# PSUM buffers of a score kernel re-dealt: shared in the first unit, one engine each, two-bank transposed tiles from the third unit on

## The chip, the cores and the metric

The kernel runs on one core of a Trainium2 chip. The metric is the device time of one execution in microseconds (us), taken as the median of several runs; lower is better. Engines are called PE (matmul), PEld (weight load, beside PE), DVE (vector), ACT (scalar), POOL (GpSimd) and SP (which here only issues transfers).

## The reference

```python
def setup_inputs():
    batch, heads, seq, dim = 8, 8, 512, 64      # q and k: float32, 16.8 MB together

def reference(q, k):
    scale = 1.0 / np.sqrt(q.shape[-1])
    return (np.einsum('bhqd,bhkd->bhqk', q, k) * scale).astype(np.float32)   # 67.1 MB
```

The output is four times the input. The matmuls contract over 64 only.

## The kernel before

The work is cut into four units of two batches each. A unit is loaded (two DMAs of 2.1 MB), cast to bf16 on POOL, transposed on PE into PSUM (the memory that PE writes to here), and copied out of PSUM by DVE and ACT into `kT` and `qz`, the operands of the score matmuls. Then 32 pairs of score matmuls follow, each into a PSUM tile of 4 KB per partition, which is scaled into one of the large SBUF buffers. (A tile of 4 KB per partition is called two-bank here, one of 2 KB one-bank.) Eight such scalings, called evacuations, fill one buffer, and one DMA of 4.19 MB stores it: 16 stores in all. The three large buffers (`big`) serve the loads and the stores alike. While unit v is scored, the transposes and copies of unit v+1 are taken in small steps between the evacuations; a step is the transposes of one tile, or one copy. Every engine runs its instructions in this program order.

```python
    big_pool = ctx.enter_context(tc.tile_pool(name="big", bufs=3))
    bf_pool = ctx.enter_context(tc.tile_pool(name="bf", bufs=6))
    tpsum_pool = ctx.enter_context(tc.tile_pool(name="tpsum", bufs=2, space=bass.MemoryType.PSUM))
    psum_pool = ctx.enter_context(tc.tile_pool(name="psum", bufs=3, space=bass.MemoryType.PSUM))
    # [cut]
    def evacuate(dst, src):
        nonlocal n_evac
        if n_evac % 6 in (0, 2, 3):
            pinned(nc.scalar.mul(out=dst, in_=src, mul=scale))
        else:
            pinned(nc.vector.tensor_scalar(out=dst, in0=src, scalar1=scale, scalar2=None,
                                           op0=mybir.AluOpType.mult))
        n_evac += 1

    def rearrange(tp, pattern, dst):          # four copies of one transposed tile
        nonlocal n_tp
        copy = (nc.vector.tensor_copy, nc.scalar.copy)[n_tp % 2]
        n_tp += 1
        for s in range(2):
            src = tp[half(s)].rearrange(pattern, n=N, h=2)
            for h in range(2):
                pinned(copy(out=dst(s, h), in_=src[:, h]))
                yield

    def transpose(v, kb, qb):
        # [cut]
        for j0 in range(0, J, 8):             # four tiles of k; four more of q follow alike
            tp = tpsum_pool.tile([P, 8, P], bf16, name="tp")
            for j in range(8):
                pinned(nc.tensor.transpose(out=tp[:, j, :], identity=identity,
                                           in_=kb[:, j0 + j].rearrange("p s d -> p (s d)")))
            yield
            yield from rearrange(tp, "d j (n h m) -> d h n m j",
                                 lambda s, h: kT[half(h), :, :, s, j0:j0 + 8])
    # [cut]
    for v in range(UNITS):
        ahead = transpose(v + 1, *cast[v + 1]) if v + 1 < UNITS else iter(())
        for t in range(TILES):
            for n, _ in enumerate(scores(v, t)):
                take(ahead, 1 + (t > 0 if v == 0 else n % 4 == 3))
```

Of the kernel before, what the change touches and what calls it, by code (L numbers as in the profile page):

```python
# [1 line left out]

# [5 lines left out]


@with_exitstack  # L10
def kernel(
    ctx: ExitStack,
    tc: tile.TileContext,
    q: bass.AP,
    k: bass.AP,
    out: bass.AP,
):






    nc = tc.nc
    B, H, S, D = q.shape
    scale = 1.0 / (D ** 0.5)
    P = 128
    UNITS = B // 2
    N = H
    M = P // (2 * H)  # L30
    R = S // M
    J = R // 2
    RO = 8
    U = S // RO
    JJ = J // RO
    IW = 8 // JJ
    TILES = N // 2

    f32 = mybir.dt.float32
    bf16 = mybir.dt.bfloat16  # L40

    q_r = q.rearrange("(v b) g (m j) d -> v (b g m) (j d)", b=2, j=R)
    k_r = k.rearrange("(v b) g (m j) d -> v (b g m) (j d)", b=2, j=R)
    out_r = out.rearrange("(v b) (t x h) (u i) k -> v (b t) (h u) x (i k)", b=2, x=2, h=2, i=RO)

    consts = ctx.enter_context(tc.tile_pool(name="consts", bufs=1))

    big_pool = ctx.enter_context(tc.tile_pool(name="big", bufs=3))
    bf_pool = ctx.enter_context(tc.tile_pool(name="bf", bufs=6))
    t_pool = ctx.enter_context(tc.tile_pool(name="t", bufs=2))  # L50
    tpsum_pool = ctx.enter_context(tc.tile_pool(name="tpsum", bufs=2, space=bass.MemoryType.PSUM))
    psum_pool = ctx.enter_context(tc.tile_pool(name="psum", bufs=3, space=bass.MemoryType.PSUM))


    pinned = tc.keep_in_program_order

    n_evac = 0
    n_tp = 0

    def evacuate(dst, src):  # L60
        nonlocal n_evac

        if n_evac % 6 in (0, 2, 3):
            pinned(nc.scalar.mul(out=dst, in_=src, mul=scale))  # L64
        else:
            pinned(nc.vector.tensor_scalar(out=dst, in0=src, scalar1=scale, scalar2=None,  # L66
                                           op0=mybir.AluOpType.mult))
        n_evac += 1

    def half(h):  # L70
        return slice(h * D, (h + 1) * D)

    def load_and_cast(v):

        xf = big_pool.tile([P, 2, 2, J * D], f32, name="big")
        both = []
        for x, src in enumerate((k_r, q_r)):
            nc.sync.dma_start(out=xf[:, x], in_=src[v].rearrange("p (s c) -> p s c", s=2))  # L78
        for x in range(2):
            xb = bf_pool.tile([P, J, 2, D], bf16, name="xb")  # L80
            for s in range(2):
                pinned(nc.gpsimd.tensor_copy(out=xb[:, :, s, :],  # L82
                                             in_=xf[:, x, s].rearrange("p (j d) -> p j d", j=J)))
            both.append(xb)
        return both

    def rearrange(tp, pattern, dst):
# [10 lines that stand above are left out]
    def transpose(v, kb, qb):  # L98


        kT = t_pool.tile([P, N, M, 2, J], bf16, name="kT")
        qz = qzs[v % 2]
        ts[v] = (kT, qz)
        for j0 in range(0, J, 8):
            tp = tpsum_pool.tile([P, 8, P], bf16, name="tp")
            for j in range(8):
                pinned(nc.tensor.transpose(out=tp[:, j, :], identity=identity,  # L107
                                           in_=kb[:, j0 + j].rearrange("p s d -> p (s d)")))
            yield
            yield from rearrange(tp, "d j (n h m) -> d h n m j",  # L110
                                 lambda s, h: kT[half(h), :, :, s, j0:j0 + 8])
        for i0 in range(0, RO, IW):
            tp = tpsum_pool.tile([P, IW, JJ, P], bf16, name="tp")
            for i in range(IW):
                for jj in range(JJ):
                    pinned(nc.tensor.transpose(out=tp[:, i, jj, :], identity=identity,  # L116
                                               in_=qb[:, RO * jj + i0 + i].rearrange("p s d -> p (s d)")))
            yield
            yield from rearrange(tp, "d i jj (n h m) -> d h i n m jj",
                                 lambda s, h: qz[half(h), i0:i0 + IW, :, h * U:(h + 1) * U]  # L120
                                 .rearrange("d i n (m s jj) -> d s i n m jj", s=2, jj=JJ)[:, s])

    def scores(v, t):

        kT, qz = ts[v]
        o = big_pool.tile([P, 2, RO, S], f32, name="big")
        for x in range(2):
            n = 2 * t + x
            for i in range(0, RO, 2):
                ps = psum_pool.tile([P, 2, S], f32, name="ps")  # L130
                for w in range(2):
                    pinned(nc.tensor.matmul(out=ps[:, w, :], lhsT=qz[:, i + w, n, :],  # L132
                                            rhs=kT[:, n].rearrange("d m s j -> d (m s j)"),
                                            start=True, stop=True))
                evacuate(o[:, x, i:i + 2, :], ps)
                yield
        nc.sync.dma_start(out=out_r[v, t], in_=o.rearrange("p x i k -> p x (i k)"))  # L137

    def take(steps, count):
        for _ in range(count):  # L140
            next(steps, None)

    identity = consts.tile([P, P], dtype=bf16)
    make_identity(nc, identity)
    qzs = [consts.tile([P, RO, N, P], bf16, name=f"qz{n}") for n in range(2)]
    for qz in qzs:
        nc.vector.memset(qz, 0.0)  # L147
    cast = [load_and_cast(v) for v in range(UNITS)]

    ts = {}  # L150
    for _ in transpose(0, *cast[0]):
        pass
    for v in range(UNITS):
        ahead = transpose(v + 1, *cast[v + 1]) if v + 1 < UNITS else iter(())
        for t in range(TILES):
            for n, _ in enumerate(scores(v, t)):

                take(ahead, 1 + (t > 0 if v == 0 else n % 4 == 3))
        for _ in ahead:
            pass  # L160


# [1 line left out]
_INS = ['q', 'k']  # L164
_OUTS = [((8, 8, 512, 512), 'float32')]


# [23 lines left out]
```

## Time and profile before

| what | value |
|---|---|
| time, median of the first 3 runs | 202.97 us (202.87 to 203.42) |
| span of the profiled run | 201.3 us |
| busy PE, DVE, ACT, POOL | 99.2, 126.4, 100.7, 30.6 us |
| bytes moved | 83.97 MB |

"Busy" is an engine's own working time. Those shares are averages over the whole span and do not say what bounds the kernel. The slices and windows do, and they are shown and read in the prediction. One idea from there is the **margin** of a store: how long before the transfer queue would run dry the store is issued. With 4.19 MB per store at 0.4295 MB/us, the queue would run dry at 41.7 us without any store, and 9.77 us later for each store issued. The margin of store number i (from 0) is 41.7 + 9.77 i (unrounded, 41.695 + 9.766 i) minus the time of its issue, read from the timeline's SP rows. While it is positive, transfers go on without a pause.

### The profile page before, as it was taken

The numbers are of one execution on the slowest core, as the hardware profiler recorded it, in microseconds if no ns is written. First come the engines' busy times: TensorE is split into PE (matmuls) and PEld (weight loads), VectorE is DVE, ScalarE is ACT, GpSimd is POOL, SyncE is SP. The second block draws the span as 40 slices with busy tenths as digits, with TensorE's granted clock in tenths as the row PEclk, the third lists the DMA queues.
The fourth block names the chain that finished last, engine by engine and source line by source line (L and its number), as shares of the span: only waits on it lengthen the run. The fifth ranks groups of instructions, "written<-read, shape, count | busy, mean of one in ns | idle before, by whom it ended". The sixth has DMA issues, their size and how long they took to land.

```text
span 201.3 us, 1456 instructions
## 1 busy us (share of the span) xinstructions
PE 99.2 (49%) x503; PEld 48.3 (24%) x512; DVE 126.4 (63%) x130; ACT 100.7 (50%) x129; POOL 30.6 (15%) x22
## 2 busy tenths in 40 slices
PE   0033366753976729463729554856535666710000
PEld 0033353321522414231315221432212222200000
DVE  6726659995989929796749796569635264530000
ACT  2016667786674856583837663856515341510000
POOL 1277777556000000000000000000000000000000
PEclk9999999998599996999975998888995857555555
DMA  6999999999999999999999999999999999999993
GB/s 205 430 443 430 420 433 440 420 407 427 433 436 425 422 443 427 430 423 440 430 423 433 433 430 427 440 430 423 433 436 430 410 446 433 420 423 433 433 427 163
DMA packets 5510, 83.97 MB, mean 417 GB/s; under 512 B 384, under 2 KB 384, under 8 KB 384
## 3 DMA queue, kind: packets, MB, share of 16 engines
q1 hardware_dynamic: 5504, 83.89, 98.1%
q8 instruction: 4, 0.07, 0.1%
q14 instruction: 2, 0.02, 0.0%
HBM read 16.78 MB, written 67.11 MB: 417 GB/s over the span
## 4 chain that ended last, share of the span: by engine, by line
DMA 63%; DVE 16%; PE 3%; POOL 3%; ACT 1%; POOLq 1%; issue 1%; SPq 0%; DVEq 0%; ACTq 0%
DMA out_dram<-big 43%; DMA big<-in_q_dram 20%; DVE big L66 12%; PE ps L132 3%; DVE qz L95 3%; POOL xb L82 3%; DVE kT L95 1%; ACT big L64 1%; POOLq L186 1%; SPq L78 0%; DVEq L66 0%; SPq L137 0%; ACTq L64 0%; POOLq L82 0%
## 5 line engine op out<-in xcount | busy, mean ns | idle before, releaser
L132 PE MATMUL ps<-kT,qz 128*128 128x512 bf16 x247 | 81.1, 450 | 55.1 <-ACT big L64 39.2
L66 DVE TENSOR_SCALAR big<-ps 128x1024 f32<-128x1024 f32 x64 | 76.3, 1222 | 39.9 <-DMA out_dram<-big 29.1
L64 ACT ACTIVATE big<-ps 128x1024 f32<-128x1024 f32 x64 | 63.7, 1023 | 57.0 <-DMA out_dram<-big 30.8
L132 PEld LDWEIGHTS <-qz 128*128 128x128 bf16 x256 | 27.5, 111 | 96.0 <-issue 83.2
L82 POOL CAST xb<-big 128x2048 bf16<-128x2048 f32 x16 | 29.9, 1896 | 17.6 <-DMA big<-in_k_dram 11.9
L95 DVE COPY kT<-tp 64x512 bf16<-64x512 bf16 x32 | 22.0, 687 | 6.3 <-PE tp L107 5.7
L95 ACT COPY kT<-tp 64x512 bf16<-64x512 bf16 x32 | 18.5, 578 | 14.7 <-PE tp L107 14.4
L95 DVE COPY qz<-tp 64x512 bf16<-64x512 bf16 x32 | 22.0, 687 | 3.1 <-PE tp L116 2.7
L95 ACT COPY qz<-tp 64x512 bf16<-64x512 bf16 x32 | 18.5, 578 | 3.9 <-PE tp L116 3.6
L107 PE MATMUL tp<-identity,xb 128*128 128x128 bf16 x128 | 12.0, 254 | 16.5 <-POOL xb L82 12.5
L116 PE MATMUL tp<-identity,xb 128*128 128x128 bf16 x128 | 12.8, 265 | 6.0 <-DVE kT L95 3.5
L107 PEld LDWEIGHTS <-xb 128*128 128x128 bf16 x128 | 10.5, 116 | 20.8 <-POOL xb L82 12.8
L116 PEld LDWEIGHTS <-xb 128*128 128x128 bf16 x128 | 11.3, 122 | 10.9 <-issue 8.9
L147 DVE MEMSET qz<- 128x4096 uint32 x2 | 6.9, 3472 | 2.5 <-PEq L175 1.7
L95 ACT ACT_TABLE_LOAD x1 | 1.3, 1283 | 0.7 <-PEq L175 0.7
masks.py:199 POOL TENSOR_SCALAR_AFFINE_SELECT identity<-identity 128x128 bf16<-128x128 bf16 x1 | 0.3, 294 | 0.1
masks.py:197 POOL MEMSET identity<- 128x128 bf16 x1 | 0.2, 205 | 0.3 <-POOLq L175 0.3
L175 POOL MEMSET const-float32-0.0<- 128x1 f32 x1 | 0.1, 99 | 0.2 <-issue 0.2
L175 POOL MEMSET const-bfloat16-1.0<- 128x1 bf16 x1 | 0.1, 102 | 0.0
L175 POOL MEMSET const-uint8-127<- 128x1 uint8 x1 | 0.1, 102 | 0.0
L175 POOL MEMSET const-float32-1.0<- 128x1 f32 x1 | 0.1, 99 | 0.0
## 6 DMA issues: line engine op xcount, KB each, us to landing
out_dram<-big SPq DMA_DIRECT2D x16, 4096.0 KB, 21.4
big<-in_k_dram SPq DMA_DIRECT2D x4, 2048.0 KB, 19.2
big<-in_q_dram SPq DMA_DIRECT2D x4, 2048.0 KB, 24.2
```

The source lines that it names most:

```text
L64: pinned(nc.scalar.mul(out=dst, in_=src, mul=scale))
L66: pinned(nc.vector.tensor_scalar(out=dst, in0=src, scalar1=scale, scalar2=None, op0=mybir.AluOpType.mult))
L82: pinned(nc.gpsimd.tensor_copy(out=xb[:, :, s, :], in_=xf[:, x, s].rearrange("p (j d) -> p j d", j=J)))
L95: pinned(copy(out=dst(s, h), in_=src[:, h]))
L107: pinned(nc.tensor.transpose(out=tp[:, j, :], identity=identity, in_=kb[:, j0 + j].rearrange("p s d -> p (s d)")))
L116: pinned(nc.tensor.transpose(out=tp[:, i, jj, :], identity=identity, in_=qb[:, RO * jj + i0 + i].rearrange("p s d -> p (s d)")))
L132: pinned(nc.tensor.matmul(out=ps[:, w, :], lhsT=qz[:, i + w, n, :], rhs=kT[:, n].rearrange("d m s j -> d (m s j)"), start=True, stop=True))
L147: nc.vector.memset(qz, 0.0)
L175: nc = _bacc.Bacc("TRN2", target_bir_lowering=False, num_devices=1)
L186: with _tile.TileContext(nc) as tc:
```

## The change

Its intent is to keep the compute engines moving. In the first unit, nothing is scored yet, so the transposes may also use the score tiles' PSUM. The evacuations go two to ACT and one to DVE, so that with three score tiles each PSUM buffer belongs to one engine. From the third unit on, a transposed tile is a two-bank one (16 transposes, copies of twice the length), and one of them takes the room of two. One cast moves from POOL to DVE. The step counts of the preparation change to match.

```diff
-        if n_evac % 6 in (0, 2, 3):
+        if n_evac % 3 < 2:
             pinned(nc.scalar.mul(out=dst, in_=src, mul=scale))
...
-                pinned(nc.gpsimd.tensor_copy(out=xb[:, :, s, :], ...
+                copy = nc.vector.tensor_copy if v == x == s == 0 else nc.gpsimd.tensor_copy
+                pinned(copy(out=xb[:, :, s, :], ...
...
+        W = 8 if v < 2 else 16
+        def transposed(rows):
+            if v == 0 and n_tp % 4 > 1:
+                tp = psum_pool.tile([P, W, P], bf16, name="ps")
+            else:
+                tp = tpsum_pool.tile([P, W, P], bf16, name="tp")
+            for w, row in enumerate(rows):
+                pinned(nc.tensor.transpose(out=tp[:, w, :], identity=identity, ...
+            return tp
-        for j0 in range(0, J, 8):
-            tp = tpsum_pool.tile([P, 8, P], bf16, name="tp")
+        for j0 in range(0, J, W):
+            tp = transposed([kb[:, j0 + j] for j in range(W)])
...
-                take(ahead, 1 + (t > 0 if v == 0 else n % 4 == 3))
+                take(ahead, 2 if v == 0 else n == 0 or n % 2)
...
+        if v == 0:
+            tpsum_pool = tp_pool(1)          # closes the pool of two one-bank tiles
```

(Cut: `tp_pool`, which opens the pool of two one-bank tiles and later the pool of one two-bank tile, and q's transposes, which change as k's do.)

More of the change, by code (lines that the diff above doesn't have):

```diff
@@ L35 @@
     JJ = J // RO
-    IW = 8 // JJ
     TILES = N // 2
@@ L50, with tp_pool @@
     t_pool = ctx.enter_context(tc.tile_pool(name="t", bufs=2))
-    tpsum_pool = ctx.enter_context(tc.tile_pool(name="tpsum", bufs=2, space=bass.MemoryType.PSUM))
     psum_pool = ctx.enter_context(tc.tile_pool(name="psum", bufs=3, space=bass.MemoryType.PSUM))
+    tp_pools = ctx.enter_context(ExitStack())
+    def tp_pool(bufs):
+        tp_pools.close()
+        return tp_pools.enter_context(tc.tile_pool(name=f"tpsum{bufs}", bufs=bufs, space=bass.MemoryType.PSUM))
     pinned = tc.keep_in_program_order
@@ L81, in load_and_cast @@
             for s in range(2):
-                pinned(nc.gpsimd.tensor_copy(out=xb[:, :, s, :],
-                                             in_=xf[:, x, s].rearrange("p (j d) -> p j d", j=J)))
+                copy = nc.vector.tensor_copy if v == x == s == 0 else nc.gpsimd.tensor_copy
+                pinned(copy(out=xb[:, :, s, :], in_=xf[:, x, s].rearrange("p (j d) -> p j d", j=J)))
             both.append(xb)
@@ L103, in transpose @@
         ts[v] = (kT, qz)
-        for j0 in range(0, J, 8):
-            tp = tpsum_pool.tile([P, 8, P], bf16, name="tp")
-            for j in range(8):
-                pinned(nc.tensor.transpose(out=tp[:, j, :], identity=identity,
-                                           in_=kb[:, j0 + j].rearrange("p s d -> p (s d)")))
+        W = 8 if v < 2 else 16
[5 more added lines that the diff above has]
+            for w, row in enumerate(rows):
+                pinned(nc.tensor.transpose(out=tp[:, w, :], identity=identity,
+                                           in_=row.rearrange("p s d -> p (s d)")))
+            return tp
+        for j0 in range(0, J, W):
+            tp = transposed([kb[:, j0 + j] for j in range(W)])
             yield
             yield from rearrange(tp, "d j (n h m) -> d h n m j",
-                                 lambda s, h: kT[half(h), :, :, s, j0:j0 + 8])
+                                 lambda s, h: kT[half(h), :, :, s, j0:j0 + W])
+        IW = W // JJ
         for i0 in range(0, RO, IW):
-            tp = tpsum_pool.tile([P, IW, JJ, P], bf16, name="tp")
-            for i in range(IW):
-                for jj in range(JJ):
-                    pinned(nc.tensor.transpose(out=tp[:, i, jj, :], identity=identity,
-                                               in_=qb[:, RO * jj + i0 + i].rearrange("p s d -> p (s d)")))
+            tp = transposed([qb[:, RO * jj + i0 + i] for i in range(IW) for jj in range(JJ)])
             yield
-            yield from rearrange(tp, "d i jj (n h m) -> d h i n m jj",
+            yield from rearrange(tp.rearrange("p (i jj) c -> p i jj c", jj=JJ),
+                                 "d i jj (n h m) -> d h i n m jj",
                                  lambda s, h: qz[half(h), i0:i0 + IW, :, h * U:(h + 1) * U]
@@ L147 @@
         nc.vector.memset(qz, 0.0)
+    tpsum_pool = tp_pool(2)
     cast = [load_and_cast(v) for v in range(UNITS)]
```

## The prediction

> **What bounds the kernel now.** I read the page's slices first, because they tell whether any one resource is full for the whole span, and then stretches of 4 us from the table of windows.
>
> ```profile
> DMA  6999999999999999999999999999999999999993
> GB/s 205 430 443 430 420 433 440 420 407 427 433 436 425 422 443 427 430 423 440 430 423 433 433 430 427 440 430 423 433 436 430 410 446 433 420 423 433 433 427 163
> HBM read 16.78 MB, written 67.11 MB: 417 GB/s over the span
> ```
>
> The 16 DMA engines are busy in every slice but the first and the last, and they move 407 to 446 GB/s in each of the 38 between. No compute engine comes near: DVE is busy 63% of the span, ACT 50%, PE 49%. The windows (length, busy time of PE, PEld, DVE, ACT and POOL, clock, DMA share, GB/s) show the two ends, the join of the loads and the stores, and a stretch with no compute:
>
> ```profile
> 0.00:4.00 4.00, 0.00 (x0) 0.00 (x0) 2.34 (x1) 1.28 (x1) 0.70 (x6) 1.00 0.57 147
> 40.00:44.00 4.00, 2.02 (x14) 1.03 (x15) 3.90 (x6) 3.36 (x6) 2.82 (x2) 1.00 1.00 406
> 184.00:188.00 4.00, 0.00 (x0) 0.00 (x0) 0.00 (x0) 0.00 (x0) 0.00 (x0) 0.50 1.00 426
> 188.00:192.00 4.00, 0.00 (x0) 0.00 (x0) 0.00 (x0) 0.00 (x0) 0.00 (x0) 0.50 1.00 426
> 196.00:200.00 4.00, 0.00 (x0) 0.00 (x0) 0.00 (x0) 0.00 (x0) 0.00 (x0) 0.50 0.54 229
> ```
>
> With every compute engine idle the transfers run at 426 GB/s, no faster than beside full compute. So the transfers hold themselves up. Budget: 147 GB/s over the first 4 us is 0.59 MB, 229 GB/s over the last window is 0.92 MB, and the rest of the 83.97 MB, 82.47 MB, goes in the 192 us between, at 0.4295 MB/us. Time not used for bytes at that rate: 4.0 - 0.59/0.4295 = 2.6 us at the start, 5.3 - 0.92/0.4295 = 3.2 us at the end of the 201.3 us span, and 4 x (430-406)/430 = 0.2 us at the join. Nothing else is left to win.
>
> Then the waits of the DMA queue on SP, and the chain of waits around the first outputs:
>
> ```profile
> SPq L137 <- DVE big L66: 147.9, 16, 20.0
> ...
> 46.96 1.85 POOLq L186
> 48.81 0.02 issue
> 48.84 1.23 DVE big L66
> ...
> 63.61 20.21 DMA out_dram<-big
> ```
>
> The 147.9 us look as if DVE's evacuation held the stores up. It doesn't: it is SP waiting for the next full buffer while the queue still holds earlier stores. The timeline gives the first six issues of stores at 38.23, 46.07, 58.31, 63.61, 71.19 and 83.01. At 0.4295 MB/us the 16.78 MB of loads are moved by 4 + (16.78-0.59)/0.4295 = 41.7 us, and each store of 4.19 MB lasts 9.8 us, so the queue would run dry at 41.7, 51.5, 61.3, 71.1, 80.8 and 90.6. The margins are 3.5, 5.4, 3.0, 7.5, 9.6 and 7.6 us. The last store is issued at 178.21, with transfers lasting to beyond 196. The kernel is bound by its transfers, with one thin place: the first three stores.
>
> **What the Trainium skill says.** "DMA: Bandwidth & Descriptors", section Where 436 GB/s comes from, puts the fabric's ceiling at 435 GB/s, and says that for HBM to SBUF some 358 binds. Here the trace differs from the second: 430 GB/s in the middle, so this kernel sits within about 1% of the first and has no rate left to gain. "SBUF — State Buffer", section SBUF: two separate sides, says that compute operations and transfers do not slow each other; the trace agrees (426 idle, 430 beside compute). "ScalarE: Activation LUTs", section What ACT_TABLE_LOAD costs, gives 186 ns + 0.833 ns per element with immediate scale: 1039 ns for 1024 elements, 612 for 512; the rows below have 1023 and 578, near enough. "VectorE: DVE Perf Modes", section The perf-mode tier table, has a float32 SBUF copy of 2048 elements at 1227 ns; the kernel before has no such copy on DVE, so the trace cannot confirm it.
>
> **The change part by part.** The rows that price it:
>
> ```profile
> L66 DVE TENSOR_SCALAR big<-ps 128x1024 f32<-128x1024 f32 x64 | 76.3, 1222 | 39.9 <-DMA out_dram<-big 29.1
> L64 ACT ACTIVATE big<-ps 128x1024 f32<-128x1024 f32 x64 | 63.7, 1023 | 57.0 <-DMA out_dram<-big 30.8
> L82 POOL CAST xb<-big 128x2048 bf16<-128x2048 f32 x16 | 29.9, 1896 | 17.6 <-DMA big<-in_k_dram 11.9
> L95 DVE COPY kT<-tp 64x512 bf16<-64x512 bf16 x32 | 22.0, 687 | 6.3 <-PE tp L107 5.7
> L95 ACT COPY kT<-tp 64x512 bf16<-64x512 bf16 x32 | 18.5, 578 | 14.7 <-PE tp L107 14.4
> ```
>
> *Evacuation two to one.* ACT takes 86 of the 128 evacuations and DVE 42: ACT 63.7 + 22 x 1.023 = 86.2 us, DVE 76.3 - 22 x 1.222 = 49.4 us. *Two-bank tiles.* For units three and four, 32 copies of 512 elements on each engine become 16 of 1024. I put such a copy at the evacuation's cost, 1.22 on DVE and 1.02 on ACT (estimates): DVE saves 32 x 0.687 - 16 x 1.22 = 2.5 us, ACT 32 x 0.578 - 16 x 1.02 = 2.2 us. *One cast moved* from POOL to DVE: +1.2 us on DVE (from the tier table), -1.9 on POOL. Sums: ACT 100.7 + 22.5 - 2.2 = 121 us, DVE 126.4 - 26.9 - 2.5 + 1.2 = 98 us. The fuller engine goes from 126 to 121 us; both stay far below the 194 us of transfers, so this is worth 0. Per steady unit the fuller engine had 16 x 1.222 + 16 x 0.687 = 30.5 us (DVE) and will have 21.3 x 1.023 + 8 x 1.02 = 30.0 us (ACT), against 4 x 9.8 = 39 us of stores. The margin hardly moves.
>
> *First unit.* Before, the casts of k run on POOL from 8.71 to 12.44, one after the other. Now one half runs on DVE, which finishes its memsets at 9.40, so k is ready near 11: 1.5 us sooner. q's casts end at 17.3, bound by its landing at 13.57, and stay. With four one-bank tiles instead of two, transposes no longer wait for copies: DVE stood idle 1.51 us between rounds. All k copies are out of the way by 17.5; q's four tiles need one transpose round (0.95 us) and two rounds of copies (2 x 2.79 us on DVE): 17.3 + 0.95 + 5.6 = 23.9, against 28.98 (DVE) and 29.38 (ACT) before, 5 us sooner. But the first output's buffer is a load buffer, free when unit two's casts end at 27.11. So the first evacuation moves from 29.41 to 27.2, and the first store from 38.23 to about 36. The queue holds loads until 41.7: worth 0, or a part of the 0.2 us dip.
>
> *Stores two and three.* The second must wait for unit three's casts (POOL, 36.9), the third for unit four's (48.81, set by a landing at 44.9); neither moves. Store three's filling took 58.31 - 48.84 = 9.5 us, with 16 steps of the next unit's transposes between its evacuations. The new schedule takes two steps from the first evacuation on, so 8 of the 40 are left for it: DVE has 3 evacuations and some 3 copies (5.7 us), ACT 5 and 4 (7.4 us). I expect its issue at 56.5 to 57, and the margin to grow from 3.0 to 4.5 us. It was never used up, so this too is worth 0. Sum of all parts: 0 to -0.2 us.
>
> **Rivals.** *The earlier start pays:* if transfers sat idle before the first store, its 2 us would come off whole, giving 201 us. For it: the dip to 406 GB/s. Against it: the DMA share is 1.00 there. *A new wait lets the queue run dry:* from unit three on a single two-bank tile serves all transposes, and PE works in order, so a late copy stalls the score matmuls behind it. Each round adds perhaps 16 transposes (1 to 2 us) and 4 copies (4 to 5 us); a buffer's fill might grow from 8 to 11 us. The margins of 7.5 us and more absorb that; only if a fill took 16 us would each store lose time, and three lost per unit would make 206 us or more. The ready-ahead copies make that unlikely. *ACT becomes the bound:* 121 us of work in 174 us before the last issue; against it. *Stores and loads collide more:* a first store issued at 36 shares engines with the last load, which would land later than 44.9 and delay the third store. The load is ahead in the queue, and a delay of 1 us fits in the margin: 203 us.
>
> **Range and chances.** I predict 202.9 us: 202.97 with at most 0.1 off. The three runs before spread over 0.55 us, so two kernels that are the same can differ by 0.5; the range is 202.2 to 203.6. Faster by 2% needs 4.06 us of the 6.0 us of unused transfer time, nearly all at the two ends, which no part touches: 1%. Slower by 2% needs the third store 3 + 4 us late or a lasting dry queue: 2%. Within 2%: 97%.
>
> **What would show it right or wrong.** Right: DMA slices unchanged at 9 with about 430 GB/s; ACT near 121 us, DVE near 98; first store issued near 36, third before 58; the last issue still near 178 and the tail unchanged. Single steps fail if a 1024-element copy costs more than an evacuation, or if the first evacuation does not move to 27. The prediction fails if a slice after the first shows the DMA share below 9, or if the rate itself, which I take as given, moves with the order of loads and stores.

## The result, and the profile after

| kernel | median | runs |
|---|---|---|
| before | 203.05 us | 202.87 to 203.42, 4 runs |
| after | 203.20 us | 203.06 to 203.36, 4 runs |

The ratio is 1.0005, 95% interval 0.9987 to 1.0023: the same. Ratios in this document are the mean time of one kernel's fast runs over that of the other's of the same rounds, so they are not quite the ratios of the medians. Where two experiments are compared with each other, their two ratios to the kernel before are divided.

The page of the changed kernel, the slices of the span and the two groups of evacuations:

```profile
DMA  6999999999999999999999999999999999999994
GB/s 205 432 426 436 426 429 439 423 397 426 436 437 419 434 432 423 436 436 429 419 439 432 419 436 442 423 423 436 439 397 426 445 423 419 419 423 442 432 426 182
...
L68 ACT ACTIVATE big<-ps 128x1024 f32<-128x1024 f32 x86 | 83.8, 1025 | 42.2 <-PE ps L144 18.1
...
L70 DVE TENSOR_SCALAR big<-ps 128x1024 f32<-128x1024 f32 x42 | 51.4, 1224 | 61.8 <-PE ps L144 37.8
```

The DMA row is as full as before. What has changed is the last column of the two groups, which names what ended the largest part of the engine's idle time. Before, it was the end of a store (lines in the prediction): ACT and DVE waited for a buffer to come free, which is the wait of a producer that is ahead. Now it is PE, with 18.1 of ACT's 42.2 us and 37.8 of DVE's 61.8: they wait for scores. PE's own waits between 60 and 160 us (for whom, us in total, times, longest) say why. First the kernel before:

```profile
PE ps L132 <- ACT big L64: 28.6, 18, 4.5
PE ps L132 <- DVE big L66: 9.8, 13, 2.0
PE tp L116 <- DVE kT L95: 0.3, 1, 0.3
```

and the changed kernel:

```profile
PE ps L144 <- ACT big L68: 9.4, 17, 2.6
PE ps L144 <- DVE big L70: 7.2, 13, 0.9
PE tp L117 <- DVE kT L99: 6.0, 2, 3.7
PE tp L117 <- ACT kT L99: 6.0, 2, 3.4
PE tp L117 <- DVE qz L99: 5.2, 2, 3.3
PE tp L117 <- ACT qz L99: 2.5, 1, 2.5
PE ps L144 <- ACT qz L99: 1.6, 1, 1.6
```

The transposes hardly waited before (0.3 us). Now they wait 19.7 us in seven waits of some 3 us. One such wait in the timeline of the changed kernel, inside the third unit's scores:

```profile
109.11 2.44 DVE L99 COPY kT<-tp 64x1024 bf16<-64x1024 bf16 x2
...
112.80 1.23 DVE L99 COPY kT<-tp 64x1024 bf16<-64x1024 bf16 x1
...
115.31 1.23 DVE L99 COPY kT<-tp 64x1024 bf16<-64x1024 bf16 x1
116.59 1.87 PE L117 MATMUL tp<-identity,xb 128*128 128x128 bf16 x16 [3.71 <-DVE kT L99]
...
118.25 2.77 PE L144 MATMUL ps<-kT,qz 128*128 128x512 bf16 x6
...
119.35 1.02 ACT L68 ACTIVATE big<-ps 128x1024 f32<-128x1024 f32 x1 [5.23 <-PE ps L144]
```

The last copy of the only transposed tile ends at 116.54. PE, which has waited 3.71 us for it, runs 16 transposes, then the scores that stand behind them in its order, and ACT has by then been idle for 5.23 us. What that does to the stores shows in their margins (us, stores 0 to 15):

```
store     0    1    2    3    4    5    6    7    8    9   10   11   12   13   14   15
before  3.5  5.4  2.9  7.4  9.6  7.5  8.8  9.8  7.7  9.0  8.8  7.8 11.0 10.0  9.6 10.0
after   6.5  4.4  5.1  9.2  9.0  7.8  8.1  6.0  4.5  2.3  1.5  0.6  3.7  8.5 11.3  9.9
```

The first store is issued at 35.24 us instead of 38.23, as intended, and its margin grows by 3 us. From store 6 to store 11 the issues come 11.3 us apart ((148.55 - 92.23) / 5), slower than the queue empties, and the margin falls to 0.6 us. Then the last unit, which prepares nothing, wins it back. The time did not move. Either both effects are hidden by the transfers, or two small real effects cancel.

### The profile page after: what moved, and what is told of

Its sections match the earlier page's. It is cut to its first block, busy times and chain, and to the rows that moved or that the text cites. A ratio compares the mean times of both kernels' runs of the same rounds, so it can differ in the third digit from the quotient of the medians.

```text
span 201.6 us, 1437 instructions
## 1 busy us (share of the span) xinstructions
PE 100.9 (50%) x512; PEld 49.1 (24%) x512; DVE 100.5 (50%) x93; ACT 118.7 (59%) x135; POOL 30.4 (15%) x21
## 5 line engine op out<-in xcount | busy, mean ns | idle before, releaser
L68 ACT ACTIVATE big<-ps 128x1024 f32<-128x1024 f32 x86 | 83.8, 1025 | 42.2 <-PE ps L144 18.1
L70 DVE TENSOR_SCALAR big<-ps 128x1024 f32<-128x1024 f32 x42 | 51.4, 1224 | 61.8 <-PE ps L144 37.8
L144 PEld LDWEIGHTS <-qz 128*128 128x128 bf16 x256 | 27.2, 109 | 85.6 <-issue 67.0
L117 PE MATMUL tp<-identity,xb 128*128 128x128 bf16 x224 | 22.4, 274 | 34.7 <-POOL xb L87 13.8
L99 DVE COPY qz<-tp 64x512 bf16<-64x512 bf16 (+1 forms) x20 | 18.0, 901 | 8.7 <-PE tp L117 8.3
L99 ACT COPY kT<-tp 64x512 bf16<-64x512 bf16 (+1 forms) x20 | 15.0, 749 | 12.5 <-PE tp L117 12.2
L99 DVE COPY kT<-tp 64x512 bf16<-64x512 bf16 (+1 forms) x20 | 18.0, 900 | 3.2 <-PE tp L117 2.9
L99 ACT COPY qz<-tp 64x512 bf16<-64x512 bf16 (+1 forms) x20 | 15.0, 749 | 4.0 <-PE tp L117 3.7
L117 PE MATMUL ps<-identity,xb 128*128 128x128 bf16 x32 | 3.1, 265 | 0.2 <-DVE kT L99 0.2
L99 DVE COPY kT<-ps 64x512 bf16<-64x512 bf16 x4 | 2.8, 688 | 0.1
L99 DVE COPY qz<-ps 64x512 bf16<-64x512 bf16 x4 | 2.8, 688 | 0.1
```

The source lines that it names most:

```text
L117: pinned(nc.tensor.transpose(out=tp[:, w, :], identity=identity, in_=row.rearrange("p s d -> p (s d)")))
L144: pinned(nc.tensor.matmul(out=ps[:, w, :], lhsT=qz[:, i + w, n, :], rhs=kT[:, n].rearrange("d m s j -> d (m s j)"), start=True, stop=True))
```

## The experiments

**Theory.** The transfers set the time. The first unit's part really makes the first store earlier, and the loads in the queue hide it. The two-bank part really makes a store cost more than the queue takes, and the margin hides it. **Rivals.** The lag while units three and four are prepared passes by itself; or it comes from the split of the evacuations; or the first unit's part gains nothing; or a gain and a loss cancel.

### Longer runs, in which a lag cannot hide: long_before, long_after, long_onebank, long_even

The same edit to each kernel: after the four units, units two to four are prepared, scored and stored again from the cast tiles still held. The result stays right (and was), with 12 more stores and no more loads.

```diff
-    for v in range(UNITS):
-        ahead = transpose(v + 1, *cast[v + 1]) if v + 1 < UNITS else iter(())
+    ORDER = [0, 1, 2, 3, 1, 2, 3]
+    for v in range(len(ORDER)):
+        ahead = transpose(v + 1, *cast[ORDER[v + 1]]) if v + 1 < len(ORDER) else iter(())
 ...
-        nc.sync.dma_start(out=out_r[v, t], ...
+        nc.sync.dma_start(out=out_r[ORDER[v], t], ...
```

long_onebank also undoes the two-bank part (`W = 8`, and the pool of two one-bank tiles stays open), but not the step counts: with one-bank tiles a unit's preparation has 40 steps, of which only 20 are then taken between the evacuations, and the other 20 follow in a lump at the end of the unit. long_even keeps the two-bank part and undoes the split (`n_evac % 6 in (0, 2, 3)`).

> The kernel before with units two to four processed a second time from the cast tiles it still holds, and stored again over the same values: 12 more stores of 4.19 MB, no more loads, right result. Theory (the stores set the time, the compute has margin in every unit): 12 x 9.77 us more than 203.05, so 320 us, and the issue of each later store stays 7 us or more ahead of the queue. Rival (compute is close to the bound already): more than 325 us.

> The changed kernel lengthened in the same way. In its trace the stores numbered 7 to 12 are issued 11.3 us apart while the queue empties one in 9.77 us, and the margin has fallen from 8.2 to 0.7 us by the twelfth. Theory (the single two-bank transposed tile makes each store cost 11.3 us wherever a unit is prepared, and only the margin hid it): 12 stores lose some 1.5 us each less the 0.7 left, so 320 + 17 = 337 us, with the DMA share below 1 after about 150 us. Rival (the lag is a passing effect of the clock and is caught up): 320 us, equal to the long kernel before.

> The long changed kernel with one-bank transposed tiles, two of them, in all units; the rest of the change stays. Theory (the single two-bank tile is the cause): 320 us, margin of 5 us or more throughout. Rival (two of three evacuations on ACT, or the fixed engine of each PSUM buffer, is the cause): about 337 us as the long changed kernel.

> The long changed kernel with the single two-bank tile but the old pattern of evacuations, half on ACT and half on DVE. Theory (the single two-bank tile is the cause): 333 us or more, since the score matmuls still wait in order behind transposes that wait for four copies. Rival (the split of two to one is the cause): 320 us.

| kernel | median | range, 4 runs | ratio to long_before | lowest margin from store 4 on |
|---|---|---|---|---|
| long_before | 322.19 us | 321.98 to 322.59 | 1 | 6.2 us |
| long_after | 331.54 us | 330.14 to 332.55 | 1.029 | -10.4 us |
| long_onebank | 322.34 us | 322.25 to 322.50 | 1.000 | 5.0 us |
| long_even | 329.12 us | 326.35 to 329.91, 3 runs | 1.019 | -8.0 us |

(A fourth run of long_even, 331.78 us, counts as slow, being over 1.5% above the fastest, and is left out. The last column extends the formula of the margin to 28 stores. A negative value says by how much the transfers have fallen behind an unbroken queue.) Two stretches of 20 us in the table of windows, DMA share and GB/s in the last two columns. The long kernel before:

```profile
184.00:204.00 20.00, 12.42 (x70) 6.07 (x68) 14.54 (x16) 12.84 (x17) 0.00 (x0) 0.83 1.01 427
244.00:264.00 20.00, 12.79 (x58) 6.03 (x58) 13.58 (x15) 13.38 (x17) 0.00 (x0) 0.84 1.00 426
```

the long changed kernel:

```profile
184.00:204.00 20.00, 10.67 (x55) 5.67 (x55) 10.99 (x9) 13.70 (x15) 0.00 (x0) 0.84 0.90 380
244.00:264.00 20.00, 12.28 (x63) 5.80 (x64) 9.62 (x9) 13.43 (x14) 0.00 (x0) 0.83 0.90 382
```

and long_onebank:

```profile
184.00:204.00 20.00, 14.21 (x64) 6.21 (x65) 13.35 (x15) 16.44 (x21) 0.00 (x0) 0.84 1.00 424
244.00:264.00 20.00, 12.55 (x64) 6.28 (x63) 12.36 (x16) 13.28 (x19) 0.00 (x0) 0.77 1.01 429
```

Once the margin is gone, the transfers pause: in the five stretches of 20 us from 164 to 264 us the DMA share is 0.90 to 0.96, and the two shown are the lowest. In these two no engine is fuller than 69%. Neither the clock nor ACT's load explains it: long_onebank moved 429 GB/s at a granted clock of 0.77, and 424 with ACT busy for 82%. The lag does not pass by itself. One-bank tiles take it away wholly, with the two-to-one split in place; the even split with the two-bank tile keeps 6.9 of the 9.4 us. So the layout with the single two-bank tile is the cause; the split alone is not, and whether it has a share in the rest these few runs do not settle.

Two limits of this. long_onebank's lump shows in its stores (store 12 comes 14.5 us after store 11, the next two after 7.1 and 6.8), so it differs from long_after also in where the copies stand. The long kernel before spreads all its steps and keeps up too, so one-bank tiles kept up with either placing. And no run has a single one-bank tile, or the two-bank tile with other step counts: whether it is that there is only one tile, its size, or the placing of its steps that hurts is not separated.

Sizes were off. long_even was expected at 333 us or more, and the long kernel before to keep margins of 7 us or more, where the lowest was 6.2. The 12 more stores of the long kernel before cost 119.4 us, not 117.2: from 196 to 316 us the rate was 426 GB/s, against 430 in the kernel before, which accounts for 12 x (4.194/0.426 - 4.194/0.430) = 1.1 of the 2.2 us; the rest is open. And the long changed kernel lost 9.4 us, not 17. Its stores 11 to 23 came (276.68 - 147.00) / 12 = 10.81 us apart, not 11.3, against the 4.194/0.426 = 9.85 us in which the queue empties one at 426 GB/s: 12 x 0.96 = 11.5, less the 2.2 us of margin left at store 11, is 9.3.

### Without the queue of loads: once_before, once_after, once_onebank

Only the first unit is loaded and cast, and all four are computed from it. The result is wrong for units two to four.

```diff
-    cast = [load_and_cast(v) for v in range(UNITS)]
+    cast = [load_and_cast(0)] * UNITS
```

> The kernel before with only the first unit loaded and cast, and all units computed from it (wrong result on purpose for units two to four): the loads that filled the queue until 41.7 us are gone, so the first store sets when the transfers begin to run through. Theory: first evacuation near 29.4 us, first store near 37.5, then 16 stores of 9.77 us and the 5 us that the normal kernel has after its last byte: 199 us, though 12.6 MB are not moved.

> The changed kernel with only the first unit loaded (wrong on purpose). Theory (the first unit's gain is real and was hidden by the loads; the two-bank tile's loss is real and was hidden by the margin): first store near 32 us, 5 us sooner than the counterpart before, but with no queue of loads to build a margin on some 6 us are lost again in the units prepared through the two-bank tile: 199 to 201 us. If only the gain is real: 193.5 us. If neither: 199 us with the first store at 37.

> As the one before, with one-bank tiles throughout (wrong on purpose). Theory: the first unit's gain shows alone: first store near 32 us, 193.5 us, 2.7% below the counterpart of the kernel before. Rival (the first unit's part is worth nothing by itself): 199 us.

| kernel | median | range, 4 runs | first store issued |
|---|---|---|---|
| once_before | 201.55 us | 200.73 to 201.58 | 38.80 us |
| once_after | 195.63 us | 195.31 to 196.64 | 32.94 us |
| once_onebank | 196.07 us | 195.35 to 196.63 | 32.52 us |

The slices' GB/s rows, first of the counterpart of the kernel before (a slice is 5.0 us), then of the changed kernel's (4.85 us):

```profile
GB/s 207 430 203 0 0 0 3 52 420 420 420 420 423 426 443 423 423 420 423 423 430 430 433 430 420 426 423 420 430 426 436 423 426 423 426 423 423 440 436 187
```

```profile
GB/s 203 432 230 0 0 3 37 399 429 432 432 432 419 429 429 412 426 422 432 426 429 426 432 429 416 422 422 432 432 429 429 426 429 405 429 429 432 432 432 179
```

Here the transfers stand idle after the first unit's load until the first store, and everything after it is one unbroken queue. The changed kernel's first store is 5.9 us sooner and the whole takes 5.9 us less (ratio 0.9638 / 0.9911 = 0.972). Most of it comes before any score is stored: the first evacuation moved from 29.20 to 23.72 us. So the first unit's part is real: in the true kernel those idle microseconds hold the loads of units two to four. It also shows how little the loads cost: leaving out 12.6 MB, 29 us of transfers at 0.4295 MB/us, saved the kernel before only 1.6 us (203.16 to 201.55), because the first store was no sooner (38.80 us against 38.23).

The expectation that the two-bank tile would take 6 us back here failed. With no buffer held by a later load, unit one's stores came as little as 5.5 us apart, which built up a margin. Counted for a queue that starts with the first store at 32.94 us, it grew from 0.3 us at store 1 to 9.6 at store 4; while units three and four were prepared it fell to 1.7 us at store 11, and no further. The loss was there and was just hidden again, though by another margin than in the true kernel. All three times came 2.1 to 2.6 us above those expected for the theory or the gain alone: the first stores were 0.5 to 1.3 us later than put, and the rate from 44 to 184 us was 426 to 427 GB/s instead of 430, some 1.1 us over 16 stores.

### The parts that gain and lose, at full length: onebank

The changed kernel with one-bank tiles throughout (the edit of long_onebank without the longer order).

> The changed kernel with one-bank transposed tiles throughout. Theory: 203.1 us, the same as both kernels, as the transfers are the same and the queue never ran dry; but the store issues keep 7 us or more ahead of the queue in units two and three, where the changed kernel fell to 0.7. Rival (the null result is a gain and a loss that cancel): 202.5 us or less here.

It took 203.40 us (202.99 to 203.55, 5 runs), ratio 1.0018, interval 1.0005 to 1.0031. The margins from store 3 on stay at 6.0 us or above (7 was expected; the lowest is store 8's, after the lump of steps at the end of a unit), so the two-bank tile's lag is gone, and the time is no better. This rules out a loss of the two-bank tile that cancelled a gain. It is even 0.2% over the kernel before, with an interval just clear of 1. One place where that could come from is the join of loads and stores. These are the windows' lines of it, the kernel before, the changed kernel, onebank:

```profile
34.00:54.00 20.00, 12.25 (x76) 6.49 (x77) 17.59 (x20) 14.73 (x21) 10.36 (x6) 0.87 1.00 420
34.00:54.00 20.00, 12.67 (x64) 5.80 (x63) 11.44 (x13) 15.68 (x22) 11.21 (x6) 0.83 1.00 422
34.00:54.00 20.00, 12.27 (x65) 5.91 (x65) 12.31 (x15) 15.74 (x22) 11.21 (x6) 0.83 1.00 419
```

Windows of 4 us within it differ more (38 to 42 us: 410, 401 and 397 GB/s), but both changed versions issue the first store some 3 us sooner, so such a window cuts the join at another place. Over the whole join the difference is worth 20 x 1 / 430 = 0.05 us. So the join does not explain the 0.2%, and its cause stays open.

### The moved cast: act_cast

In the changed kernel's trace the first cast on POOL took 3.57 us, not 1.87. Timeline of the changed kernel:

```profile
8.65 3.57 POOL L87 CAST xb<-big 128x2048 bf16<-128x2048 f32 x1 [7.35 <-DMA big<-in_k_dram]
9.32 1.16 DVE L87 CAST xb<-big 128x2048 bf16<-128x2048 f32 x1
```

```diff
-                copy = nc.vector.tensor_copy if v == x == s == 0 else nc.gpsimd.tensor_copy
+                copy = nc.scalar.copy if v == x == s == 0 else nc.gpsimd.tensor_copy
```

> The changed kernel with the one moved cast on ACT instead of DVE, to find why the first cast on POOL took 3.57 us there against 1.87 before. Theory (DVE's cast and POOL's hold each other up[...]): POOL's first cast takes 1.9 us again, ACT's about 1.9, the first transposes start near 10.7 instead of 12.28, and the time stays at 203.1 us because the first store gains nothing. Rival (POOL's cast is slowed by something else at that moment): 3.5 us again.

```profile
8.41 1.90 ACT L87 CAST xb<-big 128x2048 bf16<-128x2048 f32 x1 [6.39 <-DMA big<-in_k_dram]
8.44 1.89 POOL L87 CAST xb<-big 128x2048 bf16<-128x2048 f32 x1 [7.14 <-DMA big<-in_k_dram]
```

With its partner on ACT, POOL's cast takes 1.89 us again and the first transposes start at 10.45 instead of 12.28. The Trainium skill, "SBUF — State Buffer", section SBUF: two separate sides, says that POOL and a DVE operation in a two-port mode take a shared port pair as an exclusive lock. The run agrees that POOL's cast is held up when DVE casts beside it; that this cast ran in such a mode is not shown by a run. The first store was issued at 35.28, no sooner, since its buffer still came free only at the end of unit two's casts (first evacuation at 26.85 against 27.11). One look gave 203.03 us (one run, state unknown).

### Trying to win at the start: two_queues, split_first

The unused transfer time lies at the two ends. In two_queues (on onebank) the first q load is issued on ACT's queue; in split_first (on the kernel before) the first k load is issued in two halves on SP's and ACT's queues.

```diff
 two_queues:
+            eng = nc.scalar if v == 0 and x == 1 else nc.sync
+            eng.dma_start(out=xf[:, x], ...
 split_first:
+            if v == x == 0:
+                nc.sync.dma_start(out=xf[:, x, 0], in_=rows[:, 0])
+                nc.scalar.dma_start(out=xf[:, x, 1], in_=rows[:, 1])
```

> One-bank tiles throughout, and the first unit's q load issued on ACT's queue instead of SP's, so that the first two loads are issued at once. Theory (the unused transfer time lies at the ends; only what starts the transfers sooner can help): more than 0.59 MB in the first 4 us and 202.3 to 203.0 us. If the ramp at the start does not depend on the issuing queue: 203.1 us with 0.59 MB.

> The kernel before with one edit: the first load (k of unit one) in two halves, one issued on SP's queue and one on ACT's, all else as before. In the run with q's first load on ACT's queue the first 4 us moved 193 GB/s against 147, worth 0.43 us, but the stretch from 38 to 46 us then ran at 336 and 401 against 410 and 422. Theory (the start gains and the join of loads and stores is left as in the kernel before): 202.5 us. Rival (what the start gains is lost again at the join): 202.9 us or more.

Both expectations of a gain failed. two_queues took 203.69 us (203.61 to 203.90, 5 runs), ratio 1.0041, interval 1.0027 to 1.0054: slightly slower. Its first 4 us moved 193 GB/s instead of 152 in onebank, but k and q now shared the engines, k's cast could start only at 13.06 us instead of 8.70, and the first store came at 36.66. The join ran at 336 GB/s from 38 to 42 us and 401 from 42 to 46:

```profile
38.00:42.00 4.00, 2.87 (x17) 1.26 (x17) 3.85 (x6) 3.94 (x6) 3.44 (x2) 1.00 1.05 336
42.00:46.00 4.00, 2.62 (x22) 1.50 (x22) 3.31 (x5) 3.94 (x6) 1.14 (x2) 1.00 0.94 401
```

At 430 GB/s these 8 us would have moved as much in 1.1 us less (over 34 to 54 us the rate was 406, against 419 to 422 above), which is more than the 4 x 41 / 430 = 0.4 us gained at the start. Why the join runs so much slower in that order is not settled. In split_first, k landed as before (its cast starts at 8.66), the first 4 us moved 135 GB/s, and the time was 203.14 us (202.99 to 203.46, 5 runs), ratio 1.0006, interval 0.9992 to 1.0019. So dividing the first load between two queues did not fill the slow ramp at the start; what sets the ramp stays open, as two whole loads on two queues did move more. No version that I tried is shown to beat either kernel.

## Why the prediction was right

**The bound: right.** The DMA row is full in all slices but the two at the ends, the last store is issued at 178.25 us (178.21 before), and the time is 203.20 against 202.9 predicted. The 0.3 us between lie within the spread of the runs, 0.55 us.

**Busy times: right within 3 us.** ACT 118.7 us against 121, DVE 100.5 against 98. A copy of 1024 elements took 1.22 us on DVE and 1.00 on ACT, as put. The moved cast took 1.16 us on DVE (1.2 put). Worth nothing, as said.

**First unit and first stores: two steps failed, the rest held.** The prediction put k ready at 11, 1.5 us sooner. It was ready at 12.22, against 12.44 before: the two casts ran into each other, POOL's lasting 3.57 us. The skill's section was read and cited for transfers, and its sentence on the port shared by POOL and DVE was passed over. It cost nothing because q's landing set the next step anyway. The first evacuation came at 27.11 (27.2 predicted), the first store at 35.24 (36), the third at 56.10 (56.5 to 57), its margin 5.1 us (4.5). The second store was said to stay, but its first evacuation moved from 36.92 to 38.06, as unit three's q landed 1.15 us later (its casts start at 34.30 instead of 33.15), and its margin fell from 5.4 to 4.4; that was hidden too.

**The margin in the steady units: the step that failed.** "The margin hardly moves" was worked out from busy times alone, and it fell to 0.6 us, because PE's waits in order do not show in busy time. The prediction's own rival had the mechanism right, and its limit mis-sized. It named one two-bank tile, PE in order, score matmuls behind late copies, a fill of perhaps 11 us. The stores came 11.3 us apart. But it then said that "only if a fill took 16 us would each store lose time". That treats the margin as if each store had its own. It is one reserve, and every store made more slowly than the queue empties, 9.8 us, draws on it: 11.3 takes 1.5 us each time. The five steps from store 6 to store 11 drew it down from 8.1 to 0.6 us. The prediction of no change held because only two units are prepared in this way, with 0.6 us to spare: in this step it was luck. Three more such units cost 9.4 us (long_after). The 2% given to slower rested on that limit per store. The Trainium skill, "Perfetto Trace Analysis", section Optimization Strategy, says of the engine that should be saturated that a gap repeating on it can mean too little memory for the next tile (buffer count, tile sizes). PE is not the engine that bounds this kernel, but the reading fits it: seven waits for the copies, 19.7 us in all, became six of 6.8 us in all in the same 100 us with two one-bank tiles (onebank), though both layouts take the same 16 KB of PSUM per partition.

**The rival that the earlier start pays: rightly refused**, and now shown: 5.9 us where no loads fill the queue, nothing where they do. The rival that loads and stores collide more did not come about either: the casts that wait for the last load start at 45.11 us, against 45.07 before.

**What would make it wrong** included a rate that moves with the order of loads and stores. In the changed kernel it did not move: 422 GB/s over the join from 34 to 54 us, against 420 before. In two_queues, where the first two loads were issued at once, it fell to 406.

## What to carry to other kernels

When transfers fill the span, judge a change of the compute by the margin of each store ahead of the queue, not by the time: a stage that falls behind spends a reserve, and the time stays still until the reserve is gone. Compare the spacing of the stores with the time that the queue takes for one, and lengthen the run if the answer matters for larger inputs. Fewer and larger buffers save instructions but can serialize an engine that runs in order: two tiles of one bank kept up where one tile of two banks did not.

## What the Trainium skill lacked or had wrong

- "SBUF — State Buffer", section SBUF: two separate sides: it says that whichever operation starts first, POOL's or one of DVE in a two-port mode, gets the shared ports and the other fully blocks. Here POOL's cast started first (8.65 us) and was held up, 3.57 us instead of 1.89, while DVE's cast, started at 9.32, took 1.16 us with no wait seen; and POOL lost 1.7 us, more than the whole of DVE's cast. (POOL's spans are rough, but its end released the transposes at 12.28.)
- "DMA: Bandwidth & Descriptors", section Where 436 GB/s comes from: some 358 GB/s is said to bind between HBM and SBUF, without a condition, though the same section calls a measured 425 GB/s near the fabric's rate. Here, on one core, loads ran at 433 GB/s (4 to 34 us) and stores at 430 (54 to 196 us) in the kernel before.
- No page tells what happens where loads and stores meet: over 34 to 54 us, 420 GB/s in the kernel before, 422 in the changed one, and 406 with one load on a second queue (336 in the 4 us from 38), against 430 from 54 to 196 us.
